# Cached keys of a sample pair in one tile, a head in each half of the rows

## The chip, the core and the metric

The kernel runs on one core of one Trainium2 chip. A core has five engines that run at once, each with its own queue: TensorE (PE, with the loading of its weights, PEld, shown apart), VectorE (DVE), ScalarE (ACT), GpSimd (POOL) and SyncE (SP), which here issues all the DMAs. The metric is the device time of one execution in microseconds (us). The kernel before takes 1792.44 us, the median of three runs (1790.51 to 1794.34).

## What is computed

One layer of a streaming encoder for two request groups: a prompt of 1024 frames and a sample of 64 frames with cached keys and values. The change lies in the sample's self-attention. There are 16 heads of 64 elements: eight of kind A, which look at 512 cached rows, and eight of kind B (with a forget gate), which look at 1024 cached rows; both also look at the 64 new rows.

```python
def attend(q, k, v, bias, mask):
    scale = q.shape[-1] ** -0.5
    logits = jnp.einsum('bqhd,bkhd->bhqk', q, k).astype(jnp.float32) * scale
    if bias is not None:
        logits = logits + bias
    if mask is not None:
        logits = jnp.where(mask, logits, -jnp.inf)
    p = jax.nn.softmax(logits, axis=-1)
    return jnp.einsum('bhqk,bkhd->bqhd', p.astype(v.dtype), v)

def chunk_band_attn_sample(qa, ka, va, cache_k, cache_v, table):
    ...
    k = jnp.concatenate([cache_k, ka], axis=1)
    v = jnp.concatenate([cache_v, va], axis=1)
    ...
    return attend(qa, k, v, bias, None).reshape(b, s, h * d)
```

`forget_attn_sample` is the same with another bias and a causal mask. The rest of the layer (projection, prompt attention, output product, cross-attention into 256 memory tokens, a convolutional feed-forward block) is not touched.

## The kernel before

Every fp32 product is made of products of two parts: a number x is split into `hi`, x rounded to the fast matmul type (F32R), by ScalarE, and `lo` = x - hi, by VectorE or GpSimd. `SPLIT` (line 34) lists the three products that are kept: hi·hi, hi·lo and lo·hi.

The stages in order of time: the projection with the prompt's attention (to about 600 us); the keys and values of the memory tokens, on TensorE, with the sample's attention among them (about 600 to 711 us); the output product and the cross-attention (`project`, `Mem`, lines 1050 to 1229); the feed-forward block as a block scheme of seven products (lines 1443 and 1740).

The middle stage is the one the change touches. Its main work is `line`, a list of pieces of six matmuls each (`mem_piece`, line 668), whose weights are loaded by `load_wm`, split by `split_wm`, and whose results are finished by `mem_end` and `mem_turn`. The sample's heads go in eight pairs in the order of `SAMPLES` (line 25): pairs 4, 7, 5, 6 of kind B, then 0, 1, 3, 2 of kind A. The loop at line 988 has nine turns. Turn x loads the sample x+1 (`load`), and weaves among `PER[x]` pieces of `line` these steps: `score` and `splitv` of sample x, the transposes and sums (`turn`, `sum`, `out`) of sample x-1, and `prep` and `splitk` of sample x+1. `PER` is 4, 8, 9, 12, 6, 5, 6, 0, 0, after 15 pieces that have gone before: the last two turns have no such piece left. When `line` is empty, `open_left` (line 956) gives back the memory of this stage and loads the prompt's attention result (`mraw`, eight tiles of 512 KB, four buffers), which ScalarE and VectorE split for the first output products at line 931.

The steps of a sample, as far as the change touches them:

- `proj_sample.store` (line 359, in the first stage) writes the pair's normalised queries and keys to DRAM (`sqk`). In `qk` each head's 64 numbers stand twice, so that a later transpose puts them in both halves of the rows; all of it is stored.
- `load` (line 718) fetches `sqd` (queries and keys back), `svn`, the bias `s`, the cached keys and the cached values. The host has laid out the cached keys (`cak`, `cbk`) transposed, with a head's 64 rows twice, 128 rows in all. One tile `kraw` (three buffers) takes a head: 256 KB for kind A, 512 KB for kind B. A chunk of 512 cached values is a tile `vraw` (three buffers).
- `prep` (line 741) transposes four blocks of `sqd`, a query and a key block for each head, and multiplies them by the gain through `gained` (line 254: ScalarE writes `hi`, VectorE writes `lo`). The queries' tile `z` (one of the two `zq`) is left with the hi part in its rows 0 to 63 and the lo part in rows 64 to 127, a head at each end of its four columns of blocks, zeros in the middle two. The keys' parts are `skn0` and `skn1`.
- `splitk(h)` (line 762) splits a head's `kraw` by chunks of 512 columns into `kchi` and `kclo`.
- `score` (line 780) makes the logits of both heads in one PSUM tile, head 0 in rows 0 to 63, head 1 in rows 64 to 127. Because the contraction over 128 rows holds hi and lo of the query against the doubled key, a head needs two products (with `kchi`, with `kclo`), and the pair four for each chunk and four for the new rows, all accumulated.

The tile framework that builds the program sets the order of the instructions on each engine when it is built, apart from where an order is written out: in the trace, single products of `score` stand between single products of `mem_piece`, though the code issues a `score` in one go. All DMAs go through SP's queue, which takes them in order: one that waits for a buffer holds up those behind it.

Of the kernel before, what the change touches and what calls it, by code (L numbers as in the profile page):

```python
# [7 lines left out]
F32 = mybir.dt.float32  # L8
# [33 lines left out]
def hybrid_step(ctx: ExitStack, tc: tile.TileContext, i: dict, o: dict):  # L42
# [3 lines left out]
    def f32(ap):  # L46
        return ap.bitcast(F32)
# [17 lines left out]
    mixd = dram.tile([8, P, T], F32, name="mixd")  # L65
    sqk = dram.tile([8, S, 512], F32, name="sqk")
    sv = dram.tile([8, S, P], F32, name="sv")
# [268 lines left out]
    def proj_sample(p, subs):  # L336
# [22 lines left out]
        def store():  # L359
            vflat = vf[:S].rearrange("p h d -> p (h d)")  # L360
            cols = slice((p % 4) * P, (p % 4) * P + P)
            kout, vo, r0 = (o["ak"], o["av"], 512) if p < 4 else (o["bk"], o["bv"], T)
            nc.sync.dma_start(kout[r0:r0 + S, cols], ko[:S])
            nc.sync.dma_start(vo[r0:r0 + S, cols], vflat)
            nc.sync.dma_start(sqk[p], qk[:S].rearrange("p h a d -> p (h a d)"))
            nc.sync.dma_start(sv[p], vflat)
# [342 lines left out]
    class Sample:  # L709
# [8 lines left out]
        def load(self):  # L718
            p, n = self.p, self.ctx + S
            self.qd = mq.tile([S, 4, P], F32, name="sqd", bufs=2)  # L720
            nc.sync.dma_start(self.qd.rearrange("t h d -> t (h d)"), sqk[p])
            self.vraw = mq.tile([S, 2, 64], F32, name="svn", bufs=2)
            nc.sync.dma_start(self.vraw.rearrange("t h d -> t (h d)"), sv[p])
            b = self.s = wk.tile([P, N], F32, name="s", bufs=4)
            for h in range(2):
                r = slice(h * S, h * S + S)
                if p < 4:
                    nc.sync.dma_start(b[r, :n], toeplitz(2 * p + h, S, n))
                else:
                    nc.sync.dma_start(b[r, :n], negs[2 * (p - 4) + h:2 * (p - 4) + h + 1].broadcast_to([S, n]))  # L730
            self.kraw, self.craw, self.kc, self.vc = [], [], {}, []
            for h in range(2):
                raw = mq.tile([P, T], F32, name="kraw", bufs=3)[:, :self.ctx]
                nc.sync.dma_start(raw, self.ck[2 * (p % 4) + h])
                self.kraw.append(raw)
            for c in range(self.nc):
                raw = mq.tile([P, 4, 2, 64], F32, name="vraw", bufs=3)
                nc.sync.dma_start(raw.rearrange("p k h d -> p (k h d)"), self.cv[p % 4, c])
                self.craw.append(raw)

        def prep(self):
# [4 lines left out]
            tq = bank("tq").rearrange("p (a b) -> p a b", a=4)  # L746
            for x in range(4):
                pe.transpose(tq[:, x, :S], self.qd[:, x], ident[:S, :S])
            self.z = zq[SAMPLES.index(p) % 2]
            self.q = self.z[:, 0:4:3]  # L750
            self.kn = [mq.tile([P, 2, S], F32R, name=f"skn{x}", bufs=2) for x in range(2)]
            gained((self.q, self.z[64:, 0:4:3], tq[:, 0:2, :S], gd[:, p // 4, 0:1], LOWER),
                   (self.kn[0], self.kn[1], tq[:, 2:4, :S], gd[:, p // 4, 1:2], ALL))
            if p >= 4:
# [6 lines left out]

        def splitk(self, h):
            k = self.kraw.pop(0)
            for c in range(self.nc):
                raw = k[:, c * 512:(c + 1) * 512]
                hi = mq.tile([P, 512], F32R, name="kchi", bufs=4)
                lo = mq.tile([P, 512], F32R, name="kclo", bufs=4)
                act.copy(hi, raw)
                dve.tensor_tensor(lo, raw, f32(hi), op=ALU.subtract)
                self.kc[h, c] = hi, lo  # L770

# [8 lines left out]
        def score(self):  # L780
# [4 lines left out]
            sn = bank("tq").rearrange("p (a b) -> p a b", a=4)  # L785
            for h in range(2):
                q = self.z[:, 2 * h:2 * h + 2].rearrange("p h t -> p (h t)")
                for m in range(2):
                    first, last = h + m == 0, h + m == 2
                    for c in range(self.nc):  # L790
                        pe.matmul(sp[:, c], q, self.kc[h, c][m], start=first, stop=last)
                    pe.matmul(sn[:, 0, :S], q, self.kn[m][:, h], start=first, stop=last)
            sf = sp.rearrange("p a b -> p (a b)")
# [89 lines left out]
    smix = mq.tile([P, 8, S], F32, name="smix")  # L883
    zq = [mq.tile([P, 4, S], F32R, name=f"sq{x}") for x in range(2)]
    for x in range(2):
        pool.memset(f32(zq[x][:, 1:3]), 0.0)
    samples = [Sample(p) for p in SAMPLES]
    samples[0].load()
    step(0, [samples[0].prep, lambda: samples[0].splitk(0), lambda: samples[0].splitk(1)])
    late_left, mixes = ExitStack(), ExitStack()  # L890
# [97 lines left out]
    for x in range(len(samples) + 1):  # L988
# [9 lines left out]
        if nxt:  # L998
            fin = [nxt.prep, lambda: nxt.splitk(0), lambda: nxt.splitk(1)]
        subs = new[:1] + old[:2] + new[1:] + old[2:-1] + fin[:1] + old[-1:] + fin[1:]  # L1000
# [858 lines left out]
```

## Time and profile before

| | |
|---|---|
| median of three runs | 1792.44 us |
| the profiled execution's own time | 1793.28 us |
| its span from the first to the last instruction | 1791.5 us |
| mean granted TensorE clock | 0.989 |
| memory keys and values with the sample | about 602.7 to 711.4 us |
| HBM read, written | 155.35 MB, 45.44 MB |
| instructions in the program | 34054 |

The profile comes from one execution; its span leaves 1.78 us of its own time outside. Busy time on PE is not work at full rate: matmuls overlap, so one whose busy time is 0.28 us may be followed by the next 0.12 us later. The views used here are the table of windows (busy time of each engine in a stretch, with the granted clock and the share of the DMA engines), the groups by line, the waits (who waited for whom), and the timeline.

### The profile page before, as it was taken

To read this page: it belongs to the slowest core of one execution; us is meant where nothing else is said; L and a number is where in the kernel's file an instruction comes from. 1 tells how busy PE (TensorE), PEld (TensorE's weight loads), DVE (VectorE), ACT (ScalarE), POOL (GpSimd) and SP (SyncE) were. 2 spreads that over 40 slices of the span, in tenths; PEclk is the share of its full clock that TensorE was granted. 3 is DMA by queue.
4 is the path that set the end of the run, shared out by engine and by line. 5 is a ranking of instruction groups with operands and counts; after the bars stand their busy time and mean duration, and the time that the engine had idled before them with its cause. 6 is when DMAs were issued, how large, how long until landed. Compare 5 with 4: busy or idle time off the path is not lost.

```text
span 1791.5 us, 34054 instructions
## 1 busy us (share of the span) xinstructions
PE 1719.5 (96%) x12432; PEld 1667.8 (93%) x12432; DVE 1213.7 (68%) x2678; ACT 937.5 (52%) x2058; POOL 646.1 (36%) x1003
## 2 busy tenths in 40 slices
PE   7898999999998898999999999999999999999999
PEld 6788999999997787999999999999999999999999
DVE  5777667677677686433444379877777777677994
ACT  6756667677677577434545555333333333433332
POOL 3556657778777443443433612000000000000000
PEclk8999999999999999999999999999999999999999
DMA  7322122122112677541111562222222222894232
GB/s 251 90 66 65 55 76 78 48 74 77 49 56 87 206 260 225 163 140 54 56 52 54 162 218 94 79 73 84 85 89 75 73 73 73 268 311 146 77 118 80
DMA packets 134248, 199.87 MB, mean 112 GB/s; under 512 B 20968, under 2 KB 74088, under 8 KB 134080
## 3 DMA queue, kind: packets, MB, share of 16 engines
q1 hardware_dynamic: 134080, 197.70, 34.9%
q8 instruction: 98, 1.61, 0.4%
q14 instruction: 70, 0.57, 0.1%
HBM read 155.35 MB, written 45.44 MB: 112 GB/s over the span
## 4 chain that ended last, share of the span: by engine, by line
PE 47%; DVE 3%; issue 1%; DMA 1%; POOL 1%; ACT 1%; SPq 0%; POOLq 0%; DVEq 0%; ACTq 0%
PE W L1443 25%; PE W L1740 12%; PE pj L931 7%; PE S L1186 1%; PE tq L1222 1%; PE O L1222 1%; POOL lo L914 1%; PE PT L1209 0%; DMA raw<-in_w_down_dram 0%; DMA f<-x2d 0%; DVE lo L914 0%; PE O L1186 0%; DMA kvraw<-in_w_down_dram 0%; DMA h<-ad 0%; ACT hi L913 0%
## 5 line engine op out<-in xcount | busy, mean ns | idle before, releaser
L293 PE MATMUL pj<-whi,xhi 128*128 128x384 f32 (+1 forms) x512 | 194.9, 381 | 3.1 <-ACT xhi L130 1.8
L293 PE MATMUL pj<-wlo,xhi 128*128 128x384 f32 (+1 forms) x512 | 176.3, 344 | 2.9 <-POOL wlo L123 2.7
L293 PE MATMUL pj<-whi,xlo 128*128 128x384 f32 (+1 forms) x512 | 174.8, 341 | 0.0
L1549 POOL COPY s<-gp 128x2 f32<-128x2 f32 x22 | 15.8, 718 | 335.9 <-DVE gp L1548 335.9
L498 ACT ACTIVATE s<-s,mx 128x640 f32<-128x640 f32 (+7 forms) x128 | 94.3, 737 | 79.3 <-DVE mx L496 78.2
L1443 PE MATMUL W<-h,hi 128*128 128x272 f32 x704 | 134.4, 288 | 1.4 <-ACT qlo L1579 1.4
L1740 PE MATMUL W<-f,hi 128*128 128x272 f32 x672 | 128.5, 289 | 3.0 <-DVE f L1308 3.0
L535 DVE TENSOR_TENSOR ptl<-PT,pth 128x512 fp32r<-128x512 f32 (+2 forms) x192 | 99.6, 522 | 41.3 <-ACT pth L534 39.3
L1443 PEld LDWEIGHTS W<-h,hi 128*128 128x128 f32 x704 | 110.9, 188 | 1.7 <-ACT qlo L1579 1.6
L243 POOL TENSOR_TENSOR r<-m,mhalf 128x4 f32<-128x4 f32 (+1 forms) x72 | 74.1, 1030 | 99.5 <-DVE m L242 97.0
L1740 PEld LDWEIGHTS W<-f,hi 128*128 128x128 f32 x672 | 106.6, 190 | 3.2 <-DVE f L1308 3.2
L534 ACT CAST pth<-PT 128x512 fp32r<-128x512 f32 (+2 forms) x192 | 85.0, 448 | 42.5 <-PE PT L533 41.2
L293 PEld LDWEIGHTS pj<-whi,xhi 128*128 128x128 f32 x512 | 99.0, 193 | 4.5 <-ACT xhi L130 2.2
L293 PEld LDWEIGHTS pj<-wlo,xhi 128*128 128x128 f32 x512 | 98.7, 193 | 4.7 <-POOL wlo L123 4.7
L1443 PE MATMUL W<-h,lo 128*128 128x272 f32 x352 | 101.9, 289 | 0.0
L1307 ACT CAST hi<-raw 128x512 fp32r<-128x512 f32 x68 | 42.2, 621 | 109.4 <-PE W L1443 59.2
L293 PEld LDWEIGHTS pj<-whi,xlo 128*128 128x128 f32 x512 | 97.4, 190 | 0.5 <-DVE xlo L131 0.2
L1740 PE MATMUL W<-f,lo 128*128 128x272 f32 x336 | 97.5, 290 | 0.0
L533 PE MATMUL PT<-ident,s 128*128 128x128 f32 x528 | 90.8, 279 | 6.1 <-DVE ptl L535 5.9
L246 POOL TENSOR_SCALAR qk<-qkraw,r 128x128 f32<-128x128 f32 x256 | 91.5, 375 | 6.0
L493 PE MATMUL S<-kh,q 128*128 128x256 f32 (+1 forms) x304 | 77.7, 281 | 12.4 <-DVE mx L496 11.5
L931 PE MATMUL pj<-a,hi 128*128 128x384 f32 (+1 forms) x352 | 88.7, 335 | 0.2 <-ACT hi L913 0.2
(547 smaller groups left out, 6037.9 us busy)
## 6 DMA issues: line engine op xcount, KB each, us to landing
raw<-in_w_down_dram SPq DMA_DIRECT2D x45, 256.0 KB, 3.1
wraw<-in_w_dram SPq DMA_DIRECT2D x56, 192.0 KB, 2.4
raw<-in_w_up_dram SPq DMA_DIRECT2D x41, 256.0 KB, 2.8
h<-ad SPq DMA_DIRECT2D x32, 272.0 KB, 5.2
mwraw<-in_w_mkv_dram SPq DMA_DIRECT2D x16, 512.0 KB, 5.6
raw<-in_w_mo_dram SPq DMA_DIRECT2D x32, 256.0 KB, 3.4
kvraw<-in_w_down_dram SPq DMA_DIRECT2D x32, 256.0 KB, 3.6
ad<-t SPq DMA_DIRECT2D x22, 272.0 KB, 2.1
```

Source lines behind the costliest of these rows:

```text
L243: pool.tensor_tensor(r[:rows], m[:rows], mhalf[:rows, 0:4], op=ALU.pow)
L246: pool.tensor_scalar(qk[:rows, h], raw[:rows, h * 64:(h + 1) * 64].rearrange("p (o d) -> p o d", o=1).broadcast_to([rows, 2, 64]), r[:rows ...
L293: pe.matmul(pj[:, :nw], x2[a][:, k, t * P:(t + 1) * P], wt[k][b][:, :nw], start=n == 0, stop=n == 3 * KT - 1)
L493: pe.matmul(sp[:, a:a + (k1 - k0) * P], q, kk[:, h, src], start=m == 0, stop=m == 1)
L498: act.activation(s[:, :n], s[:, :n], ACT.Exp, bias=mx, scale=-1.0, accum_out=sm)
L533: pe.transpose(pt[:, b - ch[0]], self.s[j][:, (b - w0) * P:(b - w0 + 1) * P], ident)
L534: act.copy(hi[:, f:f + n, j], pt[:, f:f + n])
L535: dve.tensor_tensor(lo[:, f:f + n, j], pt[:, f:f + n], f32(hi[:, f:f + n, j]), op=ALU.subtract)
L931: pe.matmul(out()[:, :cn], w[a][:, k % 4], x[b][k][:, c0:c0 + cn], start=k == 0 and n == 0, stop=k == KT - 1 and n == 2)
L1307: act.copy(hi, t)
L1443: pe.matmul(w[:, z, :Q], a(p, j), rights[j][b][:, z * Q:z * Q + Q], start=fresh and begin and j == 0 and x == 0, stop=final and end and j ...
L1740: pe.matmul(ws[m][:, z, :Q], la[p][:, m * P:(m + 1) * P], ra[b][:, z * Q:z * Q + Q], start=first and y == 0 and what in opening, stop=fina ...
```

## The change

The cached keys of both heads go into one tile of 128 rows: head 0 in rows 0 to 63, head 1 in rows 64 to 127, each loaded once by its own DMA of 64 rows. The queries' tile holds the hi parts as two blocks on a diagonal among zeros, and the lo parts as another such square, so that one product serves both heads; three products (`SPLIT`) take the place of four, for each chunk and for the new rows. The key part of `sqk` is no longer doubled, so `prep` transposes two blocks and not four, and `gained` is given three items and not two. `splitk` runs once for a pair and not once for a head. `kraw` has two buffers, each for a pair, and `vraw` four and not three. The lo·lo product, which the old form had among its four, falls away.

```diff
-    sqk = dram.tile([8, S, 512], F32, name="sqk")
+    sqk = dram.tile([8, S, 4, 64], F32, name="sqk")
...
-            nc.sync.dma_start(sqk[p], qk[:S].rearrange("p h a d -> p (h a d)"))
+            nc.sync.dma_start(sqk[p], qk[:S, :, 0])
...
-            self.qd = mq.tile([S, 4, P], F32, name="sqd", bufs=2)
-            nc.sync.dma_start(self.qd.rearrange("t h d -> t (h d)"), sqk[p])
+            self.qd = mq.tile([S, 2, P], F32, name="sqd", bufs=2)
+            nc.sync.dma_start(self.qd.rearrange("t h d -> t (h d)"), sqk[p].rearrange("t h d -> t (h d)"))
...
-            self.kraw, self.craw, self.kc, self.vc = [], [], {}, []
+            self.craw, self.kc, self.vc = [], [], []
+            self.kraw = mq.tile([P, T], F32, name="kraw", bufs=2)[:, :self.ctx]
             for h in range(2):
-                raw = mq.tile([P, T], F32, name="kraw", bufs=3)[:, :self.ctx]
-                nc.sync.dma_start(raw, self.ck[2 * (p % 4) + h])
-                self.kraw.append(raw)
+                nc.sync.dma_start(self.kraw[h * 64:(h + 1) * 64], self.ck[2 * (p % 4) + h][0:64])
             for c in range(self.nc):
-                raw = mq.tile([P, 4, 2, 64], F32, name="vraw", bufs=3)
+                raw = mq.tile([P, 4, 2, 64], F32, name="vraw", bufs=4)
...
-            for x in range(4):
+            for x in range(2):
                 pe.transpose(tq[:, x, :S], self.qd[:, x], ident[:S, :S])
-            self.z = zq[SAMPLES.index(p) % 2]
-            self.q = self.z[:, 0:4:3]
-            self.kn = [mq.tile([P, 2, S], F32R, name=f"skn{x}", bufs=2) for x in range(2)]
-            gained((self.q, self.z[64:, 0:4:3], tq[:, 0:2, :S], gd[:, p // 4, 0:1], LOWER),
-                   (self.kn[0], self.kn[1], tq[:, 2:4, :S], gd[:, p // 4, 1:2], ALL))
+            self.z = z = zq[SAMPLES.index(p) % 2]
+            self.kn = [mq.tile([P, S], F32R, name=f"skn{x}", bufs=2) for x in range(2)]
+            for h in range(2):
+                r = slice(h * 64, h * 64 + 64)
+                gained((z[r, 0, h], z[r, 1, h], tq[r, 0, :S], gd[r, p // 4, 0:1], slice(0, 64)))
+            gained((self.kn[0], self.kn[1], tq[:, 1, :S], gd[:, p // 4, 1:2], ALL))
...
-        def splitk(self, h):
-            k = self.kraw.pop(0)
+        def splitk(self):
             for c in range(self.nc):
-                raw = k[:, c * 512:(c + 1) * 512]
+                raw = self.kraw[:, c * 512:(c + 1) * 512]
...
-                self.kc[h, c] = hi, lo
+                self.kc.append((hi, lo))
...
-            for h in range(2):
-                q = self.z[:, 2 * h:2 * h + 2].rearrange("p h t -> p (h t)")
-                for m in range(2):
-                    first, last = h + m == 0, h + m == 2
-                    for c in range(self.nc):
-                        pe.matmul(sp[:, c], q, self.kc[h, c][m], start=first, stop=last)
-                    pe.matmul(sn[:, 0, :S], q, self.kn[m][:, h], start=first, stop=last)
+            for m, (x, y) in enumerate(SPLIT):
+                q = self.z[:, x].rearrange("p h t -> p (h t)")
+                for c in range(self.nc):
+                    pe.matmul(sp[:, c], q, self.kc[c][y], start=m == 0, stop=m == 2)
+                pe.matmul(sn[:, 0, :S], q, self.kn[y], start=m == 0, stop=m == 2)
...
-    zq = [mq.tile([P, 4, S], F32R, name=f"sq{x}") for x in range(2)]
+    zq = [mq.tile([P, 2, 2, S], F32R, name=f"sq{x}") for x in range(2)]
     for x in range(2):
-        pool.memset(f32(zq[x][:, 1:3]), 0.0)
+        pool.memset(f32(zq[x]), 0.0)
...
-    step(0, [samples[0].prep, lambda: samples[0].splitk(0), lambda: samples[0].splitk(1)])
+    step(0, [samples[0].prep, samples[0].splitk])
...
-            fin = [nxt.prep, lambda: nxt.splitk(0), lambda: nxt.splitk(1)]
+            fin = [nxt.prep, nxt.splitk]
```

## The prediction, made before the changed kernel ran

> **What bounds the kernel now.** I read the page's busy times first, then the chain of work that ended last, then the stage of the change by a table of windows, its waits, its groups by line and its timeline.
>
> ```profile
> PE 1719.5 (96%) x12432; PEld 1667.8 (93%) x12432; DVE 1213.7 (68%) x2678; ACT 937.5 (52%) x2058; POOL 646.1 (36%) x1003
> ```
>
> PE is busy for 96% of the span, so PE's work is the first thing to count. The chain, followed back, does not reach the stage of the change, so what ends last there has to be read from windows and waits. The columns of the windows are: stretch, length, busy time of PE, PEld, DVE, ACT and POOL with instructions, granted clock, DMA share, GB/s.
>
> ```profile
> 602.70:625.00 22.30, 18.09 (x140) 16.79 (x139) 14.80 (x36) 9.75 (x30) 8.65 (x13) 1.00 0.64 184
> 625.00:640.00 15.00, 12.96 (x86) 10.73 (x85) 13.13 (x32) 12.32 (x30) 8.61 (x7) 1.00 0.92 308
> 640.00:660.00 20.00, 19.27 (x131) 16.19 (x130) 17.72 (x49) 16.36 (x42) 9.13 (x8) 1.00 0.67 214
> 660.00:680.00 20.00, 19.41 (x151) 18.11 (x152) 11.90 (x28) 13.01 (x30) 8.77 (x7) 1.00 0.77 244
> 680.00:700.40 20.40, 19.74 (x141) 17.09 (x139) 12.50 (x36) 13.78 (x36) 6.57 (x7) 1.00 0.76 224
> 700.40:711.40 11.00, 6.35 (x33) 4.26 (x31) 8.68 (x19) 9.71 (x22) 1.45 (x1) 0.91 0.76 225
> 720.00:740.00 20.00, 20.00 (x123) 19.57 (x122) 8.21 (x22) 8.04 (x19) 8.11 (x6) 1.00 0.56 166
> ```
>
> From 602.7 to 700.4 PE is busy 18.09 + 12.96 + 19.27 + 19.41 + 19.74 = 89.5 of 97.7 us: it is the bound, with 8.2 us idle, most of it before 640. From 700.4 to 711.4 it is not: no memory piece is left, PE works 6.35 of 11.0 us, and ACT (9.71) and DVE (8.68) carry the last sample and the first splits of `mraw`. After that PE is full again, so what this stage gains or loses goes through to the end unchanged. PE's waits in 602.7 to 711.4 (who waited for whom, us, times, longest):
>
> ```profile
> PE PT L704 <- DVE kv L692: 3.4, 4, 1.3
> PE S L791 <- ACT kchi L768: 1.1, 1, 1.1
> PE pj L673 <- POOL mwlo L663: 1.1, 2, 0.6
> PE pj L673 <- DVE mx L801: 0.9, 1, 0.9
> PE PT L816 <- ACT s L802: 0.8, 1, 0.8
> PE S L791 <- DVE kclo L769: 0.3, 1, 0.3
> ```
>
> Only 1.1 + 0.3 us are waits for split keys. The 3.4 us for `kv` belong to memory keys and are not touched.
>
> **PE's work.** The groups of the stage (busy us, mean ns, idle before) and one sample of kind A in the timeline:
>
> ```profile
> L791 PE MATMUL S<-kchi,sq 128*128 128x512 f32 x24 | 10.2, 446 | 1.2 <-ACT kchi L768 1.1
> L748 PE MATMUL tq<-ident,sqd 64*128 64x64 f32 x32 | 3.6, 234 | 0.1
> 682.00 0.46 PE L748 MATMUL tq<-ident,sqd 64*128 64x64 f32 x4
> ...
> 684.06 0.48 PE L791 MATMUL S<-kchi,sq 128*128 128x512 f32 x1
> 684.38 0.40 PE L791 MATMUL S<-kclo,sq 128*128 128x512 f32 x1
> 684.61 0.39 PE L791 MATMUL S<-kchi,sq 128*128 128x512 f32 x1
> ...
> 685.07 0.53 PE L792 MATMUL tq<-skn,sq 128*128 128x64 f32 x4
> 685.43 0.55 PE L816 MATMUL PT<-ident,s 128*128 128x128 f32 x3
> ```
>
> Busy times overlap, so I count from start to start. Four products of 512 columns take 684.06 to 685.07, 0.25 us each; four of 64 columns take 685.07 to 685.43, 0.09 each. The stationary operand keeps its 128 columns and the moving one its 512, so a product costs what it did. The 24 products with kchi at L791, and as many with kclo, become 36: 12 × 0.25 = 3.0 us. The 32 at L792 (four a sample) become 24: 8 × 0.09 = 0.7. The 32 transposes become 16: four take 0.46 where one takes 0.234, so each further one is (0.46 - 0.234) / 3 = 0.075, and 16 × 0.075 = 1.2. That is 4.9 us. At the least spacing here for a big product, 0.23 (684.38 to 684.61), and nothing for transposes it is 3.5; at the greatest, 0.32 (684.06 to 684.38), 5.7. The share of the last sample, about 0.5, lies after 700 us, where PE idles. **PE term: -4.4 us.**
>
> **Waits for the split keys.** ACT loses 12 casts (L768) and DVE 12 subtractions (L769); a pair is then split at half the price.
>
> ```profile
> L768 ACT CAST kchi<-kraw 128x512 fp32r<-128x512 f32 x24 | 14.1, 615 | 3.2 <-DMA kraw<-in_cbk_dram 2.9
> L769 DVE TENSOR_TENSOR kclo<-kraw,kchi 128x512 fp32r<-128x512 f32 x24 | 16.7, 720 | 3.6 <-ACT kchi L768 3.0 <-DMA kraw<-in_cak_dram 0.4
> 618.82 0.48 SPq L734 DMA_DIRECT2D kraw<-in_cbk_dram  x1
> 623.83 1.14 ACT L768 CAST kchi<-kraw 128x512 fp32r<-128x512 f32 x2 [2.94 <-DMA kraw<-in_cbk_dram]
> 621.43 1.06 SPq L734 DMA_DIRECT2D kraw<-in_cbk_dram  x2
> 629.88 2.17 ACT L768 CAST kchi<-kraw 128x512 fp32r<-128x512 f32 x4
> ...
> s<-negs SPq DMA_DIRECT2D x8, 272.0 KB, 4.5
> kraw<-in_cak_dram SPq DMA_DIRECT2D x8, 256.0 KB, 3.5
> ```
>
> The one long wait is the first sample's: its second head's load leaves SP at 618.82, behind stores of memory keys, and ACT starts that head at 623.83. Now a load brings half the bytes, but into 64 rows, and the first split needs both. The trace shows no key load of 64 rows. The nearest rows bound it: 3.5 us (256 KB into 128 rows) and 4.5 us (`negs`, 272 KB into 64 rows). The second half lands at 618.82 + 3.5 to 4.5 = 622.3 to 623.3 and both chunks are split by about 624.5, where the second head's were by 625.7. But the first head's products no longer run at 620.6. If PE's order keeps its first product there, it waits to 623.0 or 623.9, 2.3 us more than now counting the 1.1 that goes; if memory pieces come first, 1.1 + 0.3 us go. **I take -0.6, with -1.4 and +2.3 as ends**, nearer the gain, since the trace's order already sets single products of a score among memory pieces. Later loads lead by more: the second sample's leave SP at 621.43 and are cast from 629.88, 8.4 us on. There are two buffers for a pair each where three held a head and a half, and a fourth `vraw`, so SP stands less.
>
> [...]
>
> **Cover and tail.** In 625 to 640 DVE works 13.13 of 15 us and ACT 12.32, and PE waits there for `mx` and `s` (0.9 + 0.8). Eight kchi/kclo pairs fall in these early samples; I take a quarter of the 1.7, **-0.4** (0 to -1.7). After 700 us the last sample has two kclo, at L769, and the second ends just ahead of the logits' reduction:
>
> ```profile
> 702.32 0.69 DVE L769 TENSOR_TENSOR kclo<-kraw,kchi 128x512 fp32r<-128x512 f32 x1 [0.59 <-ACT kchi L768]
> 703.68 0.68 DVE L769 TENSOR_TENSOR kclo<-kraw,kchi 128x512 fp32r<-128x512 f32 x1
> 704.95 0.69 DVE L794 CUSTOM_DVE_ANT_0 s<-S,s 128x512 f32<-128x512 f32 x1 [0.40 <-PE S L791]
> ...
> 709.61 0.39 PE L841 MATMUL PT<-ident,su 128*64 128x128 f32 x1 [4.03 <-DVE su L837]
> ```
>
> One of the two goes, with its cast: the reduction can start 0.68 us earlier, at most 1.2 (at the end of the other kclo and the `ptl` after it, 703.8). What is late next is ACT, with `mraw` casts and the softmax. **-0.7** (0 to -1.2).
>
> **What is added.** `prep` gets a third ACT-DVE pair through `gained`.
>
> ```profile
> L259 ACT ACTIVATE skn<-tq,gd 128x128 fp32r<-128x128 f32 x8 | 2.9, 363 | 1.1 <-DVE sq L260 1.1
> L260 DVE SCALAR_TENSOR_TENSOR sq<-tq,gd,sq 64x128 fp32r<-64x128 f32 x8 | 2.8, 356 | 0.9 <-ACT sq L259 0.8
> L836 ACT ACTIVATE st<-O,ssum 64x64 f32<-64x64 f32 x14 | 4.3, 308 | 3.4 <-PE O L829 2.9 <-DVE su L837 0.3
> L837 DVE SCALAR_TENSOR_TENSOR su<-O,ssum,st 64x64 f32<-64x64 f32 x14 | 3.9, 280 | 1.3 <-ACT st L836 1.1
> ...
> sqk<-qk SPq DMA_DIRECT2D x8, 128.0 KB, 2.2
> ```
>
> The nearest rows of 64x64 are 308 ns (L836) and 280 (L837): three pairs are 3 × 0.59 = 1.8 us of latency where two of 0.72 are 1.4. Memory pieces on PE cover it, since `prep` comes a turn ahead of `score`; uncovered it is 0.4 × 8 = 3.0 us at most. ACT's cost of 3 × 0.31 - 2 × 0.36 = 0.2 us a sample is a quarter or less of the 0.6 to 1.2 that its casts give back. PE, sooner at its pieces, will also meet the memory weights' splits sooner (`mwlo`, 1.1 us now). For both, **+0.6** (0 to +3.0). Outside the stage, the store of `sqk` is now half the bytes in pieces of 256. [...] The memset of `zq` doubles on POOL, the least busy engine; nothing, since it stands before the first sample's `prep`.
>
> **Sum:** -4.4 - 0.6 - 0.4 - 0.7 + 0.6 = **-5.5 us**. The profiled execution took 1793.28 us, its span 1791.5; so a span of 1786.0 and a time of 1787.8 there. The median of the runs, 1792.44, lies 0.84 below that execution, which gives 1786.9, so **1787.0**.
>
> **Rivals.**
>
> - *The freed time is filled again.* PE, 5% faster through its pieces, waits for `mwlo` and for the `kv` chain (1.1 + 3.4 us of waits now) and PE's gain comes to half: -2.2 us, and the tail's gain is eaten by ACT's `mraw` casts: 1790.2. For it: ACT and DVE at 82 to 88% in 625 to 660. Against: from 660 to 700 they are at 60 to 66% and PE at 97%, and both lose work. **0.25.**
> - *The clock.* The idle time of 4.03 us before 709.61 is followed by half clock:
>
> ```profile
> 709.30:716.20 6.90, 5.71 (x18) 4.63 (x19) 5.35 (x6) 5.83 (x12) 4.75 (x3) 0.51 0.88 289
> ```
>
>   If the idle time shrinks so far that the clock stays full, up to half of PE's 5.71 us goes; PE also waits for the `mraw` splits there, so I take 2.5: 1784.5. **0.12.**
> - *Slower: the late half.* If PE's order holds a score's first product where it stands and the second half lands after it, that product blocks the pieces behind it by 2.3 us, as worked out for the first sample. It decides from the point where loads come less than about 4.5 us ahead of their score. With all four samples of kind B hit it is 4 × 2.3 - 4.4 - 0.4 = +4.4: 1796.8. Against: the second sample's lead of 8.4 us. **0.08.**
> - That the change doesn't do what it says would show as 48 products; nothing speaks for it.
>
> **How the numbers follow.** The sum has 0.55. A measurement here tells about 0.2%, 3.6 us, from no change. Faster by more holds the sum and the clock, 0.67; the same is the refilled case, 0.25; slower 0.08. The range goes from 1783.5 (the clock with the tail's end) to 1792.0 (refilled with more of the added pair), leaving out the late half.
>
> **What would show it.** 36 products at L791, 24 at L792, 16 at L748, 12 kchi and 12 kclo; the last memory piece some 5 us ahead of 700.4; the wait for kchi under 1 us; the 4.03 us before 709.61 nearer 3.3. It would be wrong if PE's wait for kchi or skn grew, if PE's idle time before 700 rose over 8.2 us, or if the order that is set on building put score's products elsewhere and moved later stages, which I have not priced.

## The result: slower by 10 us, and the profile after

The changed kernel takes 1801.53 us (median of eight runs, 1795.41 to 1804.58), the kernel before 1790.53 beside it: a ratio of 1.0058, 95% interval 1.0047 to 1.0069, some 10 us more where 5.5 less were forecast. The profiled execution took 1801.88 us, its span 1800.1. TensorE's instructions fell as counted: the groups of the stage by line (busy us, mean ns, idle before) show 36 products at L788, 24 at L789 and 16 transposes at L747 (L748 to L777 of the kernel before stand one line lower in the changed one, those from L791 on three).

```profile
L788 PE MATMUL S<-kchi,sq 128*128 128x512 f32 x24 | 9.9, 445 | 0.0
L788 PE MATMUL S<-kclo,sq 128*128 128x512 f32 x12 | 5.4, 453 | 0.8 <-DVE kclo L768 0.8
L789 PE MATMUL tq<-skn,sq 128*128 128x64 f32 x24 | 4.4, 267 | 0.9 <-DVE skn L260 0.7
...
L747 PE MATMUL tq<-ident,sqd 64*128 64x64 f32 x16 | 2.7, 247 | 0.0
```

So the work went, and the time came from elsewhere. For a comparison of stretches I take start times of matmuls from the two timelines: the first and the last of the 384 products of memory pieces, the first product of the output and the 241st. The first stage ended 2.4 us earlier after than before, but so it does in e3 below (first piece at 598.2), whose first stage is that of the kernel before: that is the chance of one execution, not the change. Behind the 241st output product 0.6 us are added. So the spans differ by 3.2 + 3.4 + 3.8 + 0.6 - 2.4 = 8.6 us.

| stretch, us | before | after | difference |
|---|---|---|---|
| memory pieces, first to last | 600.8 to 700.3: 99.5 | 598.4 to 701.1: 102.7 | +3.2 |
| tail: last piece to first output product | 11.1 | 14.5 | +3.4 |
| first 240 output products | 44.9 | 48.7 | +3.8 |

The table of windows of the changed kernel (length, busy time of PE, PEld, DVE, ACT, POOL, granted clock, DMA share, GB/s) has TensorE less busy in each stretch shown, and the granted clock under 1.00. The kernel before has 12.96 and 19.27 us busy at a clock of 1.00 in the first two (rows in the prediction) and 13.00 at 0.81 in the third; its row for the last stands behind them:

```profile
625.00:640.00 15.00, 11.97 (x65) 9.80 (x66) 11.26 (x28) 9.53 (x25) 5.89 (x5) 0.84 0.80 249
640.00:660.00 20.00, 17.31 (x109) 14.40 (x108) 15.46 (x37) 13.02 (x36) 7.43 (x7) 0.95 0.42 117
...
702.00:720.00 18.00, 11.60 (x39) 9.17 (x40) 11.50 (x22) 13.48 (x30) 5.61 (x4) 0.54 0.68 211
...
740.00:760.00 20.00, 17.87 (x101) 17.64 (x101) 6.68 (x10) 6.47 (x13) 8.98 (x9) 0.91 0.50 156
```

```profile
740.00:760.00 20.00, 20.00 (x121) 20.00 (x120) 7.34 (x11) 7.69 (x16) 11.12 (x10) 1.00 0.52 166
```

What TensorE waited for from 602.7 to 715.6 us (us in all, times, longest; the five largest):

```profile
PE PT L838 <- DVE su L834: 4.3, 2, 3.1
PE PT L704 <- DVE kv L692: 4.0, 4, 1.2
PE pj L673 <- POOL mwlo L663: 2.4, 4, 0.7
PE pj L928 <- ACT hi L910: 1.9, 1, 1.9
PE pj L673 <- DVE kv L692: 1.9, 1, 1.9
```

No wait for `kchi` is left on TensorE, and 0.8 us for `kclo` (0.3 before). The others are for `kv`, the memory keys' norm (5.9 us where it was 3.4), for `mwlo` (2.4, was 1.1) and in the tail: work that the change doesn't touch.

**The memory pieces.** The timeline of the changed kernel around the wait of 1.89 us:

```profile
631.76 1.81 POOL L776 TENSOR_TENSOR vc<-vraw,vc 128x512 fp32r<-128x512 f32 x1
...
632.34 1.25 DVE L78 TENSOR_TENSOR rsq_a<-mms,rsq_y 128x1 f32<-128x1 f32 x1
...
633.62 0.16 DVE L79 SCALAR_TENSOR_TENSOR rsq_a<-rsq_a,rsq_y 128x1 f32<-128x1 f32 x1
...
633.74 1.26 POOL L663 TENSOR_TENSOR mwlo<-mwraw,mwhi 128x512 fp32r<-128x512 f32 x1 [0.16 <-ACT mwhi L662]
633.82 1.19 DVE L80 SCALAR_TENSOR_TENSOR mr<-rsq_a,rsq_y 128x1 f32<-128x1 f32 x1
...
635.05 0.48 DVE L692 SCALAR_TENSOR_TENSOR kv<-pj,mr,gmk 128x256 f32<-128x256 f32 x1
...
635.59 0.58 PE L673 MATMUL pj<-mwhi,mhi 128*128 128x256 f32 x1 [1.89 <-DVE kv L692]
```

A step on one column of numbers takes 0.16 us at L79 and 1.25 and 1.19 at L78 and L80, and each long one ends when the GpSimd subtraction beside it does (631.76 + 1.81 = 633.57; 633.74 + 1.26 = 635.00). `kv` is then late, the PSUM tile `pj` that it reads stays taken, and the next memory piece waits 1.89 us.

**The clock.** Three stretches at half clock (granted clock 0.50) begin in or behind idle times of TensorE: 1.89 us ahead of 635.59, 1.25 us ahead of 702.84 and 2.13 us ahead of 746.52.

```profile
635.10:641.90 6.80, 6.31 (x24) 5.39 (x25) 2.46 (x9) 1.36 (x5) 0.45 (x1) 0.50 0.53 174
703.30:720.40 17.10, 11.55 (x40) 9.21 (x39) 11.04 (x19) 12.99 (x28) 6.01 (x4) 0.50 0.71 221
747.70:751.10 3.40, 3.40 (x13) 3.40 (x12) 1.84 (x2) 1.68 (x4) 3.40 (x4) 0.50 0.31 99
```

The kernel before had 6.8 us of it here (709.3 to 716.1).

**The tail.** ScalarE takes its instructions in order: in the changed kernel it idles 3.28 us ahead of `st` (709.09), and the first cast of `mraw` starts only behind that, at 709.30, though the first three loads of `mraw` left SP at 578.66 and none of its eight loads took over 6.3 us to land. Before, this cast stood ahead of the step `st` that waits for the sample's sums; now it stands behind it. First the timeline of the kernel before, then that of the changed one:

```profile
703.87 1.05 ACT L973 CAST a<-mraw 128x1024 fp32r<-128x1024 f32 x1
...
705.88 0.78 ACT L802 ACTIVATE s<-s,mx 128x576 f32<-128x576 f32 x1 [0.96 <-DVE mx L801]
...
706.65 0.29 ACT L836 ACTIVATE st<-O,ssum 64x64 f32<-64x64 f32 x1
```

```profile
709.09 0.31 ACT L833 ACTIVATE st<-O,ssum 64x64 f32<-64x64 f32 x1 [3.28 <-PE O L826]
709.30 1.04 ACT L970 CAST a<-mraw 128x1024 fp32r<-128x1024 f32 x1
...
710.25 0.77 ACT L799 ACTIVATE s<-s,mx 128x576 f32<-128x576 f32 x1
...
715.59 0.69 PE L928 MATMUL pj<-a,hi 128*128 128x384 f32 x1 [1.90 <-ACT hi L910]
```

**The output product.** SP, too, takes its DMAs in order. It now issues two weight loads (`raw`) and only then the residual (`qhi`); the second `raw` waits for a buffer, both rows together take 2.56 us, to 742.32, and the residual leaves at 742.43. The residual comes late to VectorE, and TensorE waits 2.13 us. Before, it stood between the two. First SP's rows before, then the rows of SP, VectorE and TensorE after:

```profile
735.44 0.33 SPq L905 DMA_DIRECT2D raw<-in_w_o_dram  x1
735.87 0.37 SPq L1060 DMA_DIRECT2D qhi<-in_xT_dram  x1
736.70 0.33 SPq L905 DMA_DIRECT2D raw<-in_w_o_dram  x1
```

```profile
738.68 0.42 SPq L1057 DMA_DIRECT2D qhi<-in_xT_dram  x1
...
739.76 2.56 SPq L902 DMA_DIRECT2D raw<-in_w_o_dram  x2
...
742.43 0.37 SPq L1057 DMA_DIRECT2D qhi<-in_xT_dram  x1
...
745.81 0.56 DVE L1064 TENSOR_TENSOR qhi<-pj,qhi 128x384 f32<-128x384 f32 x1 [2.63 <-DMA qhi<-in_xT_dram]
...
746.52 0.58 PE L928 MATMUL pj<-a,hi 128*128 128x384 f32 x2 [2.13 <-DVE qhi L1064]
```

All three places are places of **order**: which instruction stands ahead of which on ScalarE, SP, VectorE and GpSimd. The program's order is planned when it is built, and the edit has changed it well beyond the steps that were edited, as far as the next stage.

### The profile page after: what moved, and what is told of

Same layout as the page of the kernel before. It is cut to its first block, busy times and chain, and to the rows that moved or that the text cites. A ratio compares the mean times of both kernels' runs of the same rounds, so it can differ in the third digit from the quotient of the medians.

```text
span 1800.1 us, 33972 instructions
## 1 busy us (share of the span) xinstructions
PE 1722.7 (96%) x12396; PEld 1668.8 (93%) x12396; DVE 1211.2 (67%) x2674; ACT 932.6 (52%) x2054; POOL 647.9 (36%) x1003
## 4 chain that ended last, share of the span: by engine, by line
PE 47%; DVE 3%; DMA 2%; issue 1%; POOL 1%; ACT 1%; SPq 0%; POOLq 0%; DVEq 0%; ACTq 0%
PE W L1440 25%; PE W L1737 11%; PE pj L928 7%; PE S L1183 1%; DMA kvraw<-in_w_down_dram 1%; PE tq L1219 1%; PE O L1219 1%; POOL lo L911 1%; PE PT L1206 0%; DMA raw<-in_w_down_dram 0%; PE W L928 0%; PE O L1183 0%; DVE lo L911 0%; DVE lo L1305 0%; DVE qhi L1292 0%
## 5 line engine op out<-in xcount | busy, mean ns | idle before, releaser
L535 DVE TENSOR_TENSOR ptl<-PT,pth 128x512 fp32r<-128x512 f32 (+2 forms) x192 | 99.5, 522 | 40.5 <-ACT pth L534 38.6
L493 PE MATMUL S<-kh,q 128*128 128x256 f32 (+1 forms) x304 | 77.3, 279 | 10.6 <-DVE mx L496 9.7
```

Of the source, the lines that this page charges most:

```text
L493: pe.matmul(sp[:, a:a + (k1 - k0) * P], q, kk[:, h, src], start=m == 0, stop=m == 1)
L535: dve.tensor_tensor(lo[:, f:f + n, j], pt[:, f:f + n], f32(hi[:, f:f + n, j]), op=ALU.subtract)
```

## The experiments

The theories: **ORDER**, the new order costs the time; **HALF ROWS**, the loads into 64 rows are slow; **THIRD PAIR**, the third ScalarE-VectorE pair of `prep` is what is late. Some kernels hold an order that is written out, by this function and a list of instruction numbers for each engine (each instruction is made to depend on the one ahead of it in the list), from the first loads of this stage to the last residual load of the output product:

```python
def held_order(tc):
    code = list(tc.nc.cur_bb.bb.instructions)
    for line in HELD.values():
        for a, b in zip(line, line[1:]):
            tc.add_manual_dep(code[b], code[a].name, mybir.DependencyInfo(
                mybir.DependencyClass.NoSync, mybir.DependencyReason.DATA), reason="held")
```

In the table are the ratio to the kernel before with its 95% interval, the median, and the three stretches of each kernel's one profiled execution, measured as above. Each ratio is to executions of the kernel before taken beside that kernel; their medians go from 1789.30 to 1790.53 us. So differences between kernels are taken from the ratios, with 0.001 as 1.79 us. The stretches are of one execution, which can lie several us off the kernel's median: that of e6 is 4.9 us under it, that of e15 5.5 over it.

| kernel | ratio | median, us | pieces | tail | output |
|---|---|---|---|---|---|
| before | | 1790.53 | 99.5 | 11.1 | 44.9 |
| after | 1.0058 (1.0047 to 1.0069) | 1801.53 | 102.7 | 14.5 | 48.7 |
| e1_weave | 1.0050 (1.0036 to 1.0064) | 1798.82 | 100.4 | 13.8 | 48.3 |
| e2_old_order | 1.0046 (1.0033 to 1.0059) | 1798.29 | 105.0 | 13.0 | 46.2 |
| e3_before_two_steps | 1.0000 (0.9991 to 1.0009) | 1789.21 | 99.0 | 10.9 | 45.2 |
| e4_pair_load | 0.9977 (0.9968 to 0.9987) | 1785.79 | 92.5 | 9.9 | 45.9 |
| e5_rows64_in_e4_order | 0.9989 (0.9980 to 0.9998) | 1787.63 | 97.3 | 9.9 | 46.8 |
| e6_pair_in_after_order | 1.0050 (1.0035 to 1.0066) | 1798.87 | 99.6 | 12.7 | 47.4 |
| e7_pair_in_old_order | 1.0029 (1.0019 to 1.0040) | 1795.88 | 102.1 | 12.0 | 45.2 |
| e8_columns_in_e4_order | 0.9976 (0.9966 to 0.9986) | 1785.61 | 93.1 | 9.9 | 46.8 |
| e9_after_then_e4_tail | 1.0032 (1.0021 to 1.0043) | 1795.61 | 101.9 | 11.7 | 45.6 |
| e10_before_work_in_e4_order | 1.0028 (1.0019 to 1.0036) | 1794.21 | 104.9 | 9.8 | 46.7 |
| e11_rsq_column | 1.0035 (1.0023 to 1.0047) | 1795.46 | 96.0 | 14.0 | 48.5 |
| e12_pair_rsq_column | 0.9963 (0.9951 to 0.9975) | 1783.04 | 90.6 | 9.9 | 46.8 |
| e13_cast_first | 1.0039 (1.0026 to 1.0052) | 1797.89 | 104.1 | 13.4 | 48.6 |
| e14_qhi_first | 1.0028 (1.0018 to 1.0037) | 1795.29 | 102.8 | 14.5 | 45.0 |
| e15_before_rsq_column | 0.9986 (0.9976 to 0.9996) | 1788.26 | 101.4 | 11.1 | 45.3 |
| e16_three_repairs | 0.9999 (0.9990 to 1.0007) | 1789.66 | 95.9 | 14.1 | 45.4 |

### First: the weave, the old order, the load

```diff
# e1_weave, against the changed kernel
-            fin = [nxt.prep, nxt.splitk]
+            fin = [nxt.prep, nxt.splitk, lambda: None]
# e3_before_two_steps, against the kernel before
-            fin = [nxt.prep, lambda: nxt.splitk(0), lambda: nxt.splitk(1)]
+            fin = [nxt.prep, lambda: (nxt.splitk(0), nxt.splitk(1))]
# e4_pair_load, against the changed kernel
-            for h in range(2):
-                nc.sync.dma_start(self.kraw[h * 64:(h + 1) * 64], self.ck[2 * (p % 4) + h][0:64])
+            nc.sync.dma_start(self.kraw, self.ck[p % 4])
...
-        r[f"c{c}k"] = np.concatenate([k, k], 1)
+        r[f"c{c}k"] = k.reshape(4, 128, n)
# e2_old_order: e1_weave, with the order of the kernel before in HELD
```

> The changed kernel with an empty third step in the list fin, so that the steps of a turn are spread over the memory pieces as they were in the kernel before (three steps of the next sample, not two). No work is added or taken away. Theory ORDER (the instruction order planned anew at the build costs the 10 us): the three stretches move apart from each other, and those whose order returns give back their part; ScalarE's cast of mraw still stands behind st and SP's two raw loads still ahead of qhi, so at most the first stretch (+3.2 us) comes back: 1794 to 1802. Theory HALF ROWS (the 64-row loads are late): unchanged, 1801. Theory THIRD PAIR (the third ScalarE-VectorE pair of prep is what is late): unchanged, 1801.

> The changed kernel's work (36 products, 64-row loads, three gained pairs, deeper buffers) with the order of the kernel before written out on all five engines from the first key load to the end of the output product; a pair's splits stand where the second head's stood, the third gained pair ahead of the keys'. Theory ORDER: the 10 us go and the saved products show, 1785 to 1791; ScalarE's mraw cast ends near 704 us and the first output product starts at 707 to 711 us. Theory HALF ROWS: the work is the same, so it stays at 1798 to 1803. Theory THIRD PAIR: 1798 to 1803 as well, with the waits on skn as long as now (2.0 us on VectorE).

> The kernel before with its two splitk steps joined in one, as the changed kernel's weave has it; the work is that of the kernel before to the instruction. Theory ORDER: a new order without any new work moves the time by itself, by 2 us or more (up to +5 in the stretch of the memory pieces); the tail and SP's order of qhi and raw are as before, so not the whole 10. Theories HALF ROWS and THIRD PAIR: within 1 us of the kernel before, 1790.5.

> The changed kernel with a pair's keys laid out as 128 rows by the host, so that one load of 128 rows takes the place of two of 64. Theory HALF ROWS: the wait of 1.9 us for the first kraw shrinks to under 1 us and the first stretch's +3.2 us turns to a gain: 1793 to 1797. Theory ORDER: the load alone gives 1 us or less in the first stretch, but the order is planned anew (two mraw casts stand ahead of st, SP has qhi between the raw loads again), so the tail and the output product give back 3 to 7 us: 1793 to 1799; the split by stretches tells the two apart. Theory THIRD PAIR: 1800 to 1801.

The weave of three steps gave back little (e1), within what ORDER had expected. Two expectations of ORDER were missed. A weave of two steps costs the kernel before nothing (e3), so the joined step alone is not the cause. And the old order does not bring the old time (e2): its 1798.3 us is what HALF ROWS and THIRD PAIR had forecast, and the new work in the order of the kernel before has the longest memory pieces of all. TensorE's waits in e2 from 597 to 703 us show where the time goes:

```profile
PE S L788 <- ACT kchi L767: 4.0, 4, 1.7
...
PE S L788 <- DVE kclo L768: 2.9, 4, 1.0
PE tq L789 <- DVE skn L260: 2.2, 5, 0.6
```

It waits 6.9 us for split keys, where the kernel before waits 1.4, and 2.2 us for `skn`, for which no wait is listed there. In e2 a pair's splits stand where the second head's stood, while the pair's first product stands about where the first head's products stood; one product now needs the split of both heads. Other places for the splits in that order were not tried.

e4 came out 3.7 us under the kernel before of its own group by the medians (1789.53), 0.23% by the ratio, lower than any of the theories had it. But e4 has two things at once, another load and, through it, a third order; it can't tell ORDER from HALF ROWS.

### Second: loads and orders crossed

For this, e4's order was written out for the changed kernel (e5), and for the load of 128 rows the changed kernel's order (e6) and e2's (e7). Instruction for instruction the engines but SP have the same order as the kernel it is taken from; on SP the two loads stand for the one, or the one for the two. e8 has two loads again, each of half the columns:

```diff
# e8_columns_in_e4_order, against e5_rows64_in_e4_order
-                nc.sync.dma_start(self.kraw[h * 64:(h + 1) * 64], self.ck[2 * (p % 4) + h][0:64])
+                half = slice(h * self.ctx // 2, (h + 1) * self.ctx // 2)
+                nc.sync.dma_start(self.kraw[:, half], self.ck[p % 4][:, half])
```

> The changed kernel, its two loads of 64 rows kept, with the order of e4_pair_load written out on all engines (on SP the two loads stand where the one stood). Theory HALF ROWS: slow in spite of the order, 1796 to 1802, with the loss in the stretch of the memory pieces. Theory ORDER: as fast as e4_pair_load, 1785 to 1788.

> One load of 128 rows for a pair, in the order of the changed kernel on all engines. Theory HALF ROWS: fast, 1787 to 1793, since only the tail and SP's two raw loads ahead of qhi are left of the loss. Theory ORDER: as slow as the changed kernel, 1799 to 1802.

> One load of 128 rows for a pair, otherwise e2_old_order: the work of the change in the order of the kernel before. Theory HALF ROWS: e2_old_order's loss goes, 1785 to 1789. Theory ORDER (the old order doesn't suit the new work): stays at 1796 to 1800.

> Two loads for a pair, each of 128 rows and half the columns, in the order of e4_pair_load: as many loads and as many bytes each as in e5, but all rows. If it is the 64 rows that cost, it is as fast as e4_pair_load, 1784 to 1788; if it is a second load in SP's queue, it is slow as e5 is forecast by HALF ROWS, 1796 to 1802.

This settles the main question. With the same loads, the order makes 0.0069 of the ratio (1.0058 to 0.9989, 12 us) for 64 rows and 0.0073 (13 us) for 128 rows. With the same order, the loads make 0.0008, 0.0017 and 0.0012 (1.4, 3.0 and 2.1 us, each within the width of one interval). ORDER is right in that the order sets the time; it was wrong in that the order before is the good one for the new work. There, e7's loads of 128 rows leave TensorE 5.2 us of waits for split keys and 2.2 for `skn`, so those of e2 come in the main from the order and not from the loads. (No kernel holds the changed kernel's own order and nothing else. In e6, which differs from it in the load and in that its order is written out, the two make 1.4 us together.)

What the loads do cost is seen in the timelines of e5 and, behind it, of e8:

```profile
610.95 0.48 SPq L734 DMA_DIRECT2D kraw<-in_cbk_dram  x1
...
613.77 0.34 SPq L693 DMA_DIRECT2D out_mk_dram<-kv  x1
...
614.16 0.48 SPq L734 DMA_DIRECT2D kraw<-in_cbk_dram  x1
...
617.88 0.62 ACT L767 CAST kchi<-kraw 128x512 fp32r<-128x512 f32 x1 [1.91 <-DMA kraw<-in_cbk_dram]
...
618.55 0.51 PE L788 MATMUL S<-kchi,sq 128*128 128x512 f32 x1 [1.86 <-ACT kchi L767]
```

```profile
612.95 1.74 SPq L735 DMA_DIRECT2D kraw<-in_cbk_dram  x2
```

In e5 the second half of the first sample's keys leaves SP 3.2 us behind the first, behind a store of memory keys, and every split needs both halves: TensorE stands 1.86 us. In e8 a store doesn't come between. So this is the late half of the prediction's third rival, at one sample of four. The rows themselves are a small thing: loads of 256 KB into 64 rows (e5) landed after 3.7 us in the median of the DMA view, into 128 rows (e8) after 3.4.

```profile
kraw<-in_cbk_dram SPq DMA_DIRECT2D x8, 256.0 KB, 3.7
```

```profile
kraw<-in_cbk_dram SPq DMA_DIRECT2D x8, 256.0 KB, 3.4
```

### Third: the tail, the work, and the small steps

e9 is the changed kernel with its own order to the last memory piece and e4's behind it. e10 has the work of the kernel before in e4's order (its first head's products and splits beside the second's, `vraw` with four buffers). e11 holds the changed kernel's order, and e12 e4's, and change the form of three VectorE steps in the norm of the memory keys:

```diff
-        dve.tensor_tensor(a, ms, y, op=ALU.mult)
-        dve.scalar_tensor_tensor(a, a, -0.5, y, op0=ALU.mult, op1=ALU.mult)
-        dve.scalar_tensor_tensor(out, a, 1.5, y, op0=ALU.add, op1=ALU.mult)
+        dve.tensor_scalar(a, ms, y, None, op0=ALU.mult)
+        dve.tensor_scalar(a, a, -0.5, y, op0=ALU.mult, op1=ALU.mult)
+        dve.tensor_scalar(out, a, 1.5, y, op0=ALU.add, op1=ALU.mult)
```

> The changed kernel (64-row loads) with its own order up to the last memory piece and the order of e4_pair_load from there to the end of the output product. Theory ORDER: each stretch pays for its own order, so the memory pieces stay slow (last piece some 102.7 us after the first) and the tail and the output product are as short as in e5 (9.9 and 46.8 us against 14.5 and 48.7): 1794 to 1797. If the tail were long only because the pieces end late and the clock has dropped by then, it stays at 12 to 14.5 us: 1799 to 1802.

> The work of the kernel before (four products, four transposes, 24 splits, two 128-row loads of doubled keys, two gained pairs; vraw with four buffers) in the order of e4_pair_load. Theory ORDER (the order alone sets the time and the saved products are worth little): within 2 us of e5, 1786 to 1790. Theory WORK (the saved products are worth the 4.4 us of the prediction, and the 64-row loads some 2): 1790 to 1794, with the stretch of the memory pieces 4 to 7 us longer than the 92.5 us of e4_pair_load.

> The changed kernel, its own order held, with the three small VectorE steps of the memory keys' norm (L78, L79, L80 on 128x1) written with the second operand as a column scalar (tensor_scalar) and not as a second tensor. Theory ORDER WITH THE PORT (the order puts these steps beside GpSimd's subtractions, and a VectorE step with two tensor operands waits for GpSimd to end): none of the three takes over 0.3 us where L78 and L80 now take 1.25 and 1.19, TensorE's wait of 1.89 us for kv near 635 us falls under 0.5 and the half clock behind it may go: 1796 to 1800. If the small steps are long for another reason: 1.2 us as now, 1799 to 1802.

> e4_pair_load with its own order held and the same three steps as column scalars. No wait for kv over 1.3 us stands in its memory pieces, so little is to be had: 1783.5 to 1786. If the column form were slower on VectorE: 1787 or more.

e9: the tail's and the output product's stretches shrink by 2.8 and 3.1 us while the pieces stay slow. Each stretch pays for its own order. The tail, at 11.7 us, does not reach e5's 9.9 us.

e10: in one and the same order the old work takes 0.0039 of the ratio more than the new (7.0 us against e5; 9.1 against e4). The saved work is real. It is an upper measure, since that order was planned for the new work; its memory pieces are 7.6 us longer than e5's, and 12.4 longer than e4's, where 4 to 7 were expected.

e11: the groups of the three steps, first in the changed kernel, then in e11 (where L78 to L80 have become L79 to L81):

```profile
L78 DVE TENSOR_TENSOR rsq_a<-mms,rsq_y 128x1 f32<-128x1 f32 x8 | 4.5, 567 | 2.1 <-ACT rsq_y L77 1.9
...
L80 DVE SCALAR_TENSOR_TENSOR mr<-rsq_a,rsq_y 128x1 f32<-128x1 f32 x8 | 3.4, 425 | 0.2
...
L79 DVE SCALAR_TENSOR_TENSOR rsq_a<-rsq_a,rsq_y 128x1 f32<-128x1 f32 x8 | 2.2, 279 | 0.2
```

```profile
L80 DVE TENSOR_SCALAR rsq_a<-rsq_a,rsq_y 128x1 f32<-128x1 f32 x8 | 1.7, 212 | 0.2
L81 DVE TENSOR_SCALAR mr<-rsq_a,rsq_y 128x1 f32<-128x1 f32 x8 | 1.7, 212 | 0.2
...
L79 DVE TENSOR_SCALAR rsq_a<-mms,rsq_y 128x1 f32<-128x1 f32 x8 | 1.7, 207 | 2.1 <-ACT rsq_y L77 1.9
```

The mean of a step, over eight of each, fell from 567, 279 and 425 ns to 207, 212 and 212, with the order of every engine, GpSimd's among them, held as it was. The wait of 1.89 us is gone, the mean granted clock of the profiled execution is 0.988 (0.984 in the changed kernel's), and the pieces take 96.0 us, not 102.7. By the ratios that is 0.0023, 4.1 us. e12, the same in e4's order, is the fastest kernel of the study, 0.9963 of the kernel before; its interval overlaps that of e4, so that the three steps gain anything in that order is not shown.

### Fourth: one exchange at a time

```diff
# e13_cast_first, HELD["Activation"]: the first cast of mraw and the st ahead of it change places
# e14_qhi_first, HELD["SP"]: the second raw load and the residual load behind it change places
# e15_before_rsq_column: the kernel before, its order held, with e11's form of the three steps
# e16_three_repairs: e11 with the exchanges of e13 and e14
```

> The changed kernel, its own order held but for one exchange on ScalarE: the first cast of mraw stands ahead of the st that waits for TensorE's sums. Theory TAIL BY THE CAST: the cast ends some 4 us earlier, ScalarE's chain behind it is 1.1 us shorter, and the first output product starts 1 to 3 us earlier after the last memory piece (14.5 us now): 1798 to 1800.5. If what is late in the tail is TensorE's sums at half clock, the tail stays within 0.5 us: 1800 to 1802.

> The changed kernel, its own order held but for one exchange on SP: the fifth residual load (qhi) stands ahead of the second raw load. Theory ORDER ON SP: the wait of 2.13 us in the output product goes and the 3.41 us of half clock behind it (1.7 us), so that stretch falls from 48.7 to 44.9 to 46 us: 1797 to 1799.5. If the residual's buffer is what comes late, the wait stays: 1800 to 1802.

> The kernel before, its own order held, with the three small VectorE steps as column scalars. Its trace has two of them over 0.6 us (L78 at 606.5 us with 1.25, L80 at 648.5 with 0.65), where the changed kernel has five at 0.9 or more. Theory ORDER WITH THE PORT: the gain is 1 to 2.5 us, 1787 to 1789, under half of e11's. If the column form helps for another reason, it is as much as e11's 4 to 6 us: 1784 to 1786.

> The changed kernel with e11's column scalars and the exchanges of e13 and e14, otherwise its own order. Theory ORDER: what the single repairs give adds up, 1788 to 1793, near the kernel before or under it, though the loads of 64 rows stay. If the three give one and the same time (the one that ends last only moves), it is no better than e11: 1794 to 1797.

e14 is the cleanest: one exchange of two DMAs, and the output product's stretch falls from 48.7 to 45.0 us, to where the kernel before has it (44.9). Its timeline has the residual between the two weight loads, and the wait for `qhi` is no longer among TensorE's waits from 716 to 765 us:

```profile
740.11 0.33 SPq L902 DMA_DIRECT2D raw<-in_w_o_dram  x1
...
740.60 0.33 SPq L1057 DMA_DIRECT2D qhi<-in_xT_dram  x1
...
742.34 0.33 SPq L902 DMA_DIRECT2D raw<-in_w_o_dram  x1
```

In e13 the tail is 1.1 us shorter, of the 3.4 lost there. That the cast is worth this much is not shown: in e16, with the same exchange, the tail is 14.1 us against 14.0 in e11, and e13's interval overlaps that of the changed kernel (its ratio fell by 0.0019, 3.4 us, more than its tail shows). What the rest of the tail's order does wasn't taken apart. e15: the small steps cost the kernel before something too, 0.0014 (2.5 us). That is over half of e11's 4.1, where under half was expected, and the intervals are too wide to tell the two gains apart. (The expectation counts two steps over 0.6 us in the kernel before and five of 0.9 or more in the changed one; the traces have three, with L79 at 615.5, and six.) e16: the three repairs bring the changed kernel from 1.0058 to 0.9999, 10.6 us, with all of its work and its loads of 64 rows as they were; the single gains (4.1, 3.4 and 5.4) add up to 12.9. Against e11, the two exchanges give 0.0036 (6.4 us) here, where e14's alone gives 5.4.

## Why the prediction was wrong

- **The step that failed is that every term was priced in the order of the kernel before, as if the work in it only became less.** The text's last sentence names half of this: the order that is set on building, which could move later stages, "which I have not priced". Against the order of e4 that is worth 12 us (e5 against the changed kernel), more than twice the sum of all that was priced; against the order of the kernel before it is 2.1 us, with overlapping intervals (e2). The other half the text doesn't name: held in the order in which it was priced (e2), the new work is 8.2 us slower than the kernel before, where the sum has 5.5 less. In e2's execution the memory pieces are 5.5 us longer, with 7.7 us more of waits for split keys and `skn`, the tail 1.9 and the output product 1.3. So less work in an order made for other work did not save its time, and neither of the two orders suited it.
- **The PE term (-4.4)** was right in its counts (36, 24, 16) and in its direction; in one order (e10 against e5) the new work is 7.0 us ahead, with the splits in it, and that is an upper measure. Against the kernel before in its own order, e5 is 2.0 us ahead.
- **The split keys (-0.6, from -1.4 to +2.3).** In the changed kernel TensorE's waits went from 1.4 to 0.8 us, the -0.6 of the forecast, in a new order; ScalarE there still waits 1.9 us for the first sample's keys. In the order that the term was worked out in (e2) they are 5.5 us longer, over twice the upper end. In e5 the wait for the first sample is 1.86 us, and the loads cost 1.4 to 3.0 us in all. The rival of the late half had the mechanism right and its place right for the first sample in e5. In e2 TensorE waits for `kchi` four times, but the halves of a load aren't the reason for most of it, since e7 has one load and keeps three of the four.
- **Cover (-0.4)** had the wrong sign. Less work on ScalarE and VectorE did not bring the waits of 625 to 640 down; two of VectorE's small steps (1.25 and 1.19 us) fell beside GpSimd's subtractions, and the stretch got a wait of 1.89 us and 6.8 us of half clock.
- **The tail (-0.7)** had the wrong sign, +3.4. The sentence "what is late next is ACT, with `mraw` casts and the softmax" named the right engine, but took the place of the first cast ahead of `st` as given. How much of the 3.4 is the cast's stays open (e13 and e16).
- **What is added (+0.6).** The waits on `skn` are 0.7 us on TensorE, and 2.2 in e2 and e7, within the range; THIRD PAIR was not tested by itself and is not needed for the 10 us, since e4, e8 and e12 have the third pair and are faster than the kernel before. The wait for `mwlo` rose by 1.3 us. The stores of `sqk`, half the bytes in pieces of 256, landed after 2.1 us in the median (2.2 before), and the sum has no term for them. The new numbers of buffers were not tested by themselves.
- **The output product** was put at nothing, as a stage that the change doesn't reach. It lost 3.8 us, of which one exchange on SP gives 3.7 back (e14).
- **The clock** was a rival only as a gain. It came as a loss, 27 us at half clock in the three stretches where there had been 6.8; what these cost by themselves was not measured.
- **Two slips of the text** move nothing: 0.4 × 8 is 3.2 and not 3.0, and three buffers of a head each held a pair and a half, not a head and a half.

## What to carry to other kernels

Where a framework plans the order, an edit's price has two parts, the work and the new order, and the second can be the larger: compare the engines' orders far beyond the stage that was edited, above all what now stands behind a waiting instruction on an engine or a queue that takes its work in order, as the cast did on ScalarE (709.30, behind a wait of 3.28 us) and the residual on SP (742.43, behind two `raw` rows of 2.56 us). Before an edit is given up as slow, hold its work in another order, or exchange two instructions: here the same work spans 1787.6 to 1801.5 us. And the order that was good for the old work need not be good for the new (e2).

## What the runs showed of the hardware

In the changed kernel a VectorE step on one column with two tensor operands takes 0.16 us alone and up to 1.25 beside a GpSimd subtraction; the one at 633.82 takes 1.19 and ends at 635.01, where the subtraction beside it ends at 635.00. In e11, with the second operand as a column scalar and the order of the changed kernel held, the three steps take 0.21 us in the mean of their eight places each (207, 212 and 212 ns). Why the one form is held up and the other not is shown by no run; the port in the name of e11's theory is the author's guess at it.

The half clock came with idle times of TensorE far shorter than itself: 1.89 us of idle ahead of 635.59 go with 6.8 us of it in the changed kernel (from 635.1 on), while e6, with the same wait of 1.89 us ahead of 633.76, kept full clock (1.00) in the stretch behind it, as its window shows:

```profile
633.70:640.50 6.80, 6.68 (x43) 5.54 (x44) 4.35 (x18) 4.16 (x14) 0.46 (x1) 1.00 0.62 200
```

So the price of an idle time can't be had from its length alone, and a single execution's stretches carry a chance (e6's execution lies 4.9 us under its kernel's median, e15's 5.5 over) that the medians of several runs even out.
